# Heads as one pipeline with the gate inside, values stored through the input rows' buffers, and three engines kept in written order

## The chip, the core and the metric

The kernel runs on one core of a Trainium2 chip. The core has five engines that work side by side and meet through semaphores: PE (TensorE, the matrix products), DVE (VectorE), ACT (ScalarE), POOL (GpSimd) and SP (SyncE, which here issues the DMAs). The matrix products write to PSUM, of which this kernel uses eight banks of 128 x 512 float32; everything else works on SBUF. Each engine takes its instructions in the order in which they stand in its own queue, so an instruction that waits holds up all that stand behind it on that engine. The metric is the time of one execution on the device in microseconds (us), lower is better.

## The reference, cut to what matters

One encoder layer on x (1, 1024, 1024): a gMLP branch A, an attention branch B with eight heads of 128 and three dilated windows, two gates, an output product and a norm.

```
h = rms_norm(x, g_pre)
u_a, v_a, z_a, q_b, k_b, v_b, z_b, gate_a, gate_b = split(h @ w_in)
y_a = spatial_gating(gelu(u_a), gelu(v_a), ln_g, ln_b, w_s, b_s) * silu(z_a)
y_b = mixture_of_dilations(q_b, k_b, v_b) * silu(z_b)   # windows (128,1), (512,4), (2048,16)
m = sigmoid(gate_a) * (y_a @ w_pa) + sigmoid(gate_b) * (y_b @ w_pb)
out = x + rms_norm(m @ w_o, g_post)
```

## The kernel before

All products run in float32r as three matmuls, high by high, high by low and low by high. To get the two parts, ACT copies a tile (`wh_...`, `..h`) and DVE or POOL subtracts the copy from the source (`wl_...`, `..l`): `split` (L158) for activations, `operand` (L103) for weights.

The program has four stages. **Start** (L202 to L345): eight row tiles of x (`xt`, six buffers) are normed and transposed, and the values v_b are formed in two column blocks `cb` of 512. `v_out` (L249) splits each 128 x 512 bank of values into `vh` and `vl` and stores both to DRAM; `vh` lies in one of the two `ws` buffers, `vl` in one of two of its own. **Projections** (L347 to L575): all other columns of w_in, by a scheme with seven products for a 2 x 2 block (`seven`, L369); the sums of weight tiles that it needs are formed on DVE, the first two (`s1`, `s2`) in the same two `ws` buffers (`weight_operands`, L351, L364). The first of these groups are the gates `g0`, whose first product `g0p` needs no sum and whose second needs `s2`. The gating z_b goes to DRAM (`z_d`). **Attention** (L576 to L912): for each head `h`, `queries_keys` loads and splits q and k; `scores` makes 16 score tiles of 128 x 256 in eight pairs (`sc` banks, PE), DVE adds the bias and finds the row extreme in one instruction (L661, into `st` and `own`), and ACT takes the exponential with its sum (L665). `exchange` (L669) moves maxima and sums between partitions, half 0 on POOL and half 1 on DVE, 16 small copies each (`oth`). `normalise` (L682) makes the factors (`nm`), partly through an exponential on ACT (`dd`), and `scale` (L699) applies them to `st`. `weigh` (L712) then runs nine stages; each transposes scaled weights on PE (`pb`, `pa`, `pe` banks), splits them (`pth`, `ptl`), and, two stages later (`LAG` = 2), multiplies them with the values (`pr`, `pc` banks). After the ninth stage the last two are finished, the parts are added (L803) and the head's output goes to DRAM (`o_d`).

Between all this stand the products of branch A with w_pa, cut into 256 steps of three matmuls each (`mlp_products`, L834; banks `pa`, L857 to L859), which the loop over the heads deals out: `BESIDE` says how many steps follow each stage, `PAIRS` how many score pairs of the next head. **Tail** (L913 to L1014): `gated_heads` (L917) loads o and z of two heads at a time (two `o` buffers, one `z` buffer), POOL multiplies them, and the product is split into `yh`, `yl`; the steps that are left run beside it. Then come the products with w_pb (L977 to L979) and w_o (L1008 to L1010).

A scheduler decides the order in the engines' queues: it takes the written program as priorities and moves an instruction ahead when it finds it ready in its own estimate, buffers included.

Of the kernel before, what the change touches and what calls it, by code (L numbers as in the profile page):

```python
# [9 lines left out]
F32 = mybir.dt.float32  # L10
F32R = mybir.dt.float32r
# [12 lines left out]
H = 8  # L24
# [12 lines left out]
def tile_hybrid_encoder(  # L37
# [164 lines left out]
    with tc.tile_pool(name="start", bufs=1) as sp:  # L202
# [44 lines left out]
                transposed(hT[j][b], i, xs, f"xT{c}{j}")  # L247

        def v_out(c, cb, ps):  # L249
            vh = wpool.tile([P, 512], F32R, tag="ws", bufs=2, name=f"vh{cb}{c}")  # L250
            vl = sp.tile([P, 512], F32R, tag="vl", bufs=2, name=f"vl{cb}{c}")
            split(vh, vl, ps)
            for t, d in ((vh, v_hi), (vl, v_lo)):
                stored.append(nc.sync.dma_start(d[c * P:(c + 1) * P, 512 * cb:512 * (cb + 1)], f32(t)))
# [321 lines left out]
    with tc.tile_pool(name="heads", bufs=1) as hp, tc.tile_pool(name="attn", bufs=1) as ap:  # L576
        def queries_keys(h, res):

            def pair(nm, shape):
                return [hp.tile([P] + shape, F32R, tag=f"{nm}{s}", name=f"{nm}{s}{h}") for s in "hl"]  # L580

            res["qr"], res["qc"], res["kr"] = pair("qr", [4, 256]), pair("qc", [8, P]), pair("kr", [4, 256])
            for b in range(2):
                t = wpool.tile([P, 512], F32, tag="ws", bufs=2, name=f"q{h}{b}")
                nc.sync.dma_start(t, q_d[h][:, 512 * b:512 * (b + 1)])
                split(*[w[:, :, b * P:(b + 1) * P] for w in res["qr"]], t.rearrange("p (j r) -> p r j", r=4))
                split(*[w[:, 4 * b:4 * b + 4, :].rearrange("p a (r i) -> p a r i", r=4) for w in res["qc"]],
                      t.rearrange("p (a i r) -> p a r i", a=4, r=4), nc.gpsimd)
                yield
            for s in range(2):  # L590
                nc.sync.dma_start(f32(res["kr"][s]), k_d[h][:, s])
                yield
            for x, terms, shape in (("ta", alibi_a, [P, 256]), ("te", alibi_e, [P, 2, 192]), ("tb", alibi_b, [P, 384])):
                res[x] = hp.tile(shape, F32, tag=x, name=f"{x}{h}")
                nc.sync.dma_start(res[x], terms[h])

        def residue_values(h, res):

            res["vb"] = []
            for s, vd in enumerate((v_hi, v_lo)):  # L600
# [21 lines left out]
        def scores(h, res):  # L622
# [3 lines left out]
            qr, qc, kr, ta, te, tb = [res[n] for n in ("qr", "qc", "kr", "ta", "te", "tb")]  # L626
            own = res["own"] = hp.tile([P, 2, 8, 2], F32, tag="own", bufs=2, name=f"own{h}")
            wts = res["wts"] = {}
            order = [(1, (i, i + 1)) for i in (0, 2, 4, 6)] + [(0, (0, 7)), (0, (1, 2)), (0, (3, 4)), (0, (5, 6))]
            for half, pair in order:  # L630
                ps = bank("sc", f"sc{h}{half}{pair[0]}").rearrange("p (t n) -> p t n", t=2)
                st = (hp if half else ap).tile([P, 2, 256], F32, tag=f"st{half}", bufs=8 if half else 6, name=f"st{h}{half}{pair[0]}")
                n = 256
                for t, idx in enumerate(pair):
                    if half:
# [74 lines left out]
                                                           [(0, 5), (0, 6)], []]  # L710

        def weigh(h, res):  # L712


            va, ve, vb, wts = [res[n] for n in ("va", "ve", "vb", "wts")]
# [73 lines left out]
            for i, stage in enumerate([residue(r) for r in range(4)] + [chunk(1), chunk(3), ends(), chunk(5), chunk(7)]):  # L789
# [79 lines left out]
        ya = {}  # L869
        take(mlp_tiles(0, 0, ya))  # L870
        steps = mlp_products(ya)
        heads = [{} for _ in range(H + 1)]
        take(queries_keys(0, heads[0]))
        take(steps, 8)
        residue_values(0, heads[0])
        chunk_values(0, heads[0])
        for _ in scores(0, heads[0]):
            take(steps, 1)
        take(exchange(0, heads[0], 0))
        take(exchange(0, heads[0], 1))  # L880
        normalise(0, heads[0])
        for tile_ in TILES[0] + TILES[1]:
            scale(heads[0], *tile_)
        for _ in queries_keys(1, heads[1]):
            take(steps, 3)
        for h in range(H):
            more = h + 1 < H
            pairs = scores(h + 1, heads[h + 1]) if more else iter(())
            ahead = queries_keys(h + 2, heads[h + 2]) if h + 2 < H else iter(())
            for i, _ in enumerate(weigh(h, heads[h])):  # L890
                take(pairs, PAIRS[i])
                take(steps, BESIDE[i])
                if i == 3 and more:
                    residue_values(h + 1, heads[h + 1])
                if more and i == 3:
                    take(exchange(h + 1, heads[h + 1], 0))
                    late = exchange(h + 1, heads[h + 1], 1)
                if more and i in (5, 6):
                    take(late, 1)
                if more and i == 7:  # L900
                    normalise(h + 1, heads[h + 1])
                if more and i == 8:
                    for tile_ in TILES[0] + TILES[1]:
                        scale(heads[h + 1], *tile_)
                if i > 4:
                    take(ahead, 1)
            if more:
                chunk_values(h + 1, heads[h + 1])
            take(ahead)
            take(steps, BESIDE[9])  # L910


    with tc.tile_pool(name="tail", bufs=1) as tp:  # L913

        y = {}

        def gated_heads(h, b):  # L917

            bs = slice(512 * b, 512 * (b + 1))
            o, z = [tp.tile([P, 2, 512], F32, tag=t, bufs=n, name=f"{t}{h}{b}") for t, n in (("o", 2), ("z", 1))]  # L920
            for t, src in ((o, o_d), (z, z_d)):
                nc.sync.dma_start(t, src[h:h + 2, :, bs].rearrange("k p n -> p k n"))
            for i in range(2):
                y[h + i, b] = [tp.tile([P, 512], F32R, name=f"y{s}{h + i}{b}") for s in "hl"]
                nc.gpsimd.tensor_tensor(o[:, i, :], o[:, i, :], z[:, i, :], ALU.mult)  # L925
                split(*y[h + i, b], o[:, i, :])
                yield

        ready = (_ for h in range(0, H, 2) for b in range(2) for _ in gated_heads(h, b))
        wb = {}  # L930
        for i in range(16):
            take(ready, 1)
# [130 lines left out]
```

## Time and profile before

| | us |
|---|---|
| median of 3 runs | 1597.32 (1597.07 to 1600.4) |
| the profiled execution's own time | 1596.76 |
| its span in the trace | 1595.0 |
| PE busy | 1519.5 (95%) |
| DVE busy | 882.6 (55%) |
| POOL busy | 769.4 (48%) |
| ACT busy | 689.7 (43%) |
| start ends, projections begin | about 135 |
| first transpose of head 0 | 1059.6 |
| first transpose of head 7 | 1332.7 |
| first load of o in the tail | 1362.8 |

A row of a list of groups has the line and engine, what is written from what, the shape, the count, then the busy time, the mean of one in ns, and the idle time of the engine just before them with what ended it. A row of the timeline has the start, the duration, the engine and the instruction, and in brackets the idle time before it. A row of the windows has, for a stretch of the span, each engine's busy time and number of instructions, then the granted clock of PE as a share of full speed. PE's matmuls are pipelined: one is shown as 0.39 us long, and the next may start before it ends.

### The profile page before, as it was taken

What the parts mean: (1) busy time and instruction counts of PE and PEld (TensorE: products, weight loads), DVE (VectorE), ACT (ScalarE), POOL (GpSimd) and SP (SyncE); (2) the same over time, 40 slices, a digit from 0 to 9 for tenths busy, and PEclk for the clock granted to TensorE, in tenths of its full rate; (3) what the DMA queues carried; (4) which work ended last, traced back from release to release, by engine and by line L of the source; (5) the groups of instructions that cost most, each with busy time, mean ns of one, the idle gap of its engine ahead of it and who ended that gap; (6) DMA issues with size and microseconds to landing.
All of it is one profiled execution on the core that took longest, in us unless ns stands there. A gap on an engine that the chain in (4) does not pass through costs nothing. (4 is left out here: it accounts for less than half of the span.)

```text
span 1595.0 us, 22762 instructions
## 1 busy us (share of the span) xinstructions
PE 1519.5 (95%) x7863; PEld 1277.7 (80%) x7863; DVE 882.6 (55%) x1706; ACT 689.7 (43%) x1315; POOL 769.4 (48%) x703
## 2 busy tenths in 40 slices
PE   8998999999999999999999999989998989979998
PEld 4786999988888888788788888778787767758886
DVE  5723444476675665857564655577777575232112
ACT  5522433343433434343444444677766565221111
POOL 2413544465555555555555555454444443664132
PEclk9999999999999999999999999999999989989999
DMA  8445333334534443636344443586666657785531
GB/s 258 157 166 177 117 103 107 111 126 132 165 122 149 130 154 106 184 101 188 110 146 136 131 138 123 188 234 196 207 186 187 205 161 206 223 248 175 198 106 66
DMA packets 247812, 252.16 MB, mean 158 GB/s; under 512 B 14184, under 2 KB 187272, under 8 KB 247440
## 3 DMA queue, kind: packets, MB, share of 16 engines
q1 hardware_dynamic: 247328, 249.88, 49.9%
q8 instruction: 62, 1.02, 0.3%
q10 hardware_dynamic: 368, 0.82, 0.2%
q14 instruction: 54, 0.44, 0.1%
HBM read 174.10 MB, written 76.55 MB: 157 GB/s over the span
## 5 line engine op out<-in xcount | busy, mean ns | idle before, releaser
L108 POOL TENSOR_TENSOR wl_pa<-wr_pa,wh_pa 128x512 fp32r<-128x512 f32 x56 | 73.7, 1322 | 98.1 <-ACT wh_pa L106 89.5
L512 DVE TENSOR_SCALAR vn<-vn,mean,rstd 128x128 f32<-128x128 f32 x128 | 57.1, 500 | 35.1 <-DMA vn<-v_d 34.8
L665 ACT ACTIVATE st<-st,own 128x256 f32<-128x256 f32 (+1 forms) x128 | 62.9, 492 | 24.7 <-DVE own L661 24.3
L977 PE MATMUL pb<-yh,wh_pb 128*128 128x512 f32 x128 | 50.6, 396 | 10.2 <-ACT yh L159 10.2
L978 PE MATMUL pb<-yl,wh_pb 128*128 128x512 f32 x128 | 50.8, 397 | 1.5 <-DVE yl L160 1.4
L106 ACT ACTIVATE wh_pa<-wr_pa 128x512 fp32r<-128x512 f32 x64 | 38.9, 624 | 28.8 <-PE pa L858 16.0
L678 DVE COPY oth<-own 32x4 f32<-32x4 f32 x128 | 47.3, 369 | 5.6 <-ACT st L665 3.5
L979 PE MATMUL pb<-yh,wl_pb 128*128 128x512 f32 x128 | 50.3, 393 | 0.0
L678 POOL COPY oth<-own 32x4 f32<-32x4 f32 x128 | 27.2, 212 | 38.5 <-ACT st L665 33.5
L981 POOL TENSOR_TENSOR mb<-thb,mb 128x512 f32<-128x512 f32 x16 | 20.6, 1288 | 45.7 <-DVE thb L980 36.2
L1012 ACT ACTIVATE sq<-o 128x512 f32<-128x512 f32 x16 | 9.6, 598 | 74.6 <-PE o L1010 74.6
L160 POOL TENSOR_TENSOR vl<-vn,vh 128x512 fp32r<-128x512 f32 x32 | 41.3, 1290 | 0.8 <-ACT vh L159 0.8
L160 DVE TENSOR_TENSOR yl<-o,yh 128x512 fp32r<-128x512 f32 x16 | 18.2, 1135 | 39.4 <-ACT yh L159 38.7
L992 DVE TENSOR_TENSOR sso<-sso 128x1 f32<-128x1 f32 x8 | 1.3, 159 | 67.6 <-ACT sq L1012 67.6
L160 POOL TENSOR_TENSOR qcl<-q,qch 128x512 fp32r<-128x512 f32 x16 | 25.8, 1621 | 26.0 <-ACT qch L159 26.0
L977 PEld LDWEIGHTS pb<-yh,wh_pb 128*128 128x128 f32 x128 | 24.4, 191 | 16.1 <-ACT yh L159 11.0
L160 DVE TENSOR_TENSOR vl<-vb,vh 128x512 fp32r<-128x512 f32 x16 | 10.9, 688 | 44.0 <-ACT vh L159 36.2
L661 DVE CUSTOM_DVE_ANT_0 st<-sc,tb 128x256 f32<-128x256 f32 x64 | 24.9, 419 | 17.7 <-PE sc L660 10.3
L165 POOL TENSOR_TENSOR sso<-sso,mhalf 128x1 f32<-128x1 f32 x8 | 4.4, 550 | 59.1 <-DVE sso L164 59.1
L658 PE MATMUL sc<-krh,qch 128*128 128x256 f32 (+1 forms) x80 | 24.6, 309 | 8.2 <-DVE own L661 7.6
L108 POOL TENSOR_TENSOR wl_wos<-wr_wos,wh_wos 128x512 fp32r<-128x512 f32 x16 | 20.7, 1294 | 22.8 <-ACT wh_wos L106 22.8
L160 DVE TENSOR_TENSOR ptla<-pa,ptha 128x512 fp32r<-128x512 f32 (+1 forms) x32 | 19.8, 619 | 20.1 <-ACT ptha L159 19.9
(2640 smaller groups left out, 5857.3 us busy)
## 6 DMA issues: line engine op xcount, KB each, us to landing
wr_pa<-in_w_proj_a_dram SPq DMA_DIRECT2D x32, 512.0 KB, 5.1
wr_g<-in_w_in_dram SPq DMA_DIRECT2D x16, 512.0 KB, 3.6
wr_va<-in_w_in_dram SPq DMA_DIRECT2D x16, 512.0 KB, 3.7
wr_u<-in_w_in_dram SPq DMA_DIRECT2D x16, 512.0 KB, 4.4
wr_z<-in_w_in_dram SPq DMA_DIRECT2D x16, 512.0 KB, 4.3
vn<-v_d SPq DMA_DIRECT2D x32, 256.0 KB, 2.8
y_d<-s SPq DMA_DIRECT2D x32, 256.0 KB, 3.0
wr_yf<-y_d SPq DMA_DIRECT2D x16, 512.0 KB, 6.6
```

Of the source, the lines that this page charges most:

```text
L106: nc.scalar.activation(hi, src, AF.Copy)
L108: low.tensor_tensor(lo, src, f32(hi), ALU.subtract)
L160: low.tensor_tensor(lo, src, f32(hi), ALU.subtract)
L512: nc.vector.tensor_scalar(vn[:, c, :], vn[:, c, :], mean[:, 4 * b + c, 0:1], rstd[:, 4 * b + c:4 * b + c + 1], op0=ALU.subtract, op1=ALU.mult)
L658: nc.tensor.matmul(dst, lhs[0], rhs[0], start=True, stop=False)
L661: nc.vector.tensor_tensor_reduce(st[:, t, :n], ps[:, t, :n], bias, -1.0, -NEG, ALU.add, ALU.min, own[:, half, idx, 0:1])
L665: nc.scalar.activation(st[:, t, :n], st[:, t, :n], AF.Exp, bias=own[:, half, idx, 0:1], scale=-1.0, accum_out=own[:, half, idx, 1:2])
L678: (nc.gpsimd, nc.vector)[half].tensor_copy(dst, src)
L977: nc.tensor.matmul(ps, lh, rh, start=(k == 0), stop=False)
L978: nc.tensor.matmul(ps, lh, rl, start=False, stop=False)
L979: nc.tensor.matmul(ps, ll, rh, start=False, stop=(k == KT - 1))
L981: nc.gpsimd.tensor_tensor(ma, th, ma, ALU.add)
```

## The change

Four things are changed.

- In the start, the values of the second column block go into one tile of 128 x 2 x 512 in the `xt` buffers of the input rows, not into `ws` and `vl`.
- In the attention, the last two stages of a head are finished in the first two stages of the next head's loop, not at the end of its own; each stage takes its score pairs one by one between the steps; the pairs come in another order, `exchange` and `normalise` stand a stage later, and the steps per head go from 22 to 24.
- `weigh` also loads z of its head and POOL multiplies o with it before o is stored; the tail loads only the product and splits it, every other one with POOL.
- From the first head on, PE, DVE and ACT keep the order in which the program is written; POOL and SP are still placed by the scheduler. The score tiles `st` get 7 and 7 buffers, not 8 and 6.

```
 def v_out(c, cb, ps):
-    vh = wpool.tile([P, 512], F32R, tag="ws", bufs=2, name=f"vh{cb}{c}")
-    vl = sp.tile([P, 512], F32R, tag="vl", bufs=2, name=f"vl{cb}{c}")
+    if cb:
+        vhl = sp.tile([P, 2, 512], F32R, tag="xt", bufs=6, name=f"vhl{c}")
+        vh, vl = vhl[:, 0, :], vhl[:, 1, :]
+    else:
+        vh = wpool.tile([P, 512], F32R, tag="ws", bufs=2, name=f"vh{c}")
+        vl = sp.tile([P, 512], F32R, tag="vl", bufs=2, name=f"vl{c}")
...
-    order = [(1, (i, i + 1)) for i in (0, 2, 4, 6)] + [(0, (0, 7)), (0, (1, 2)), (0, (3, 4)), (0, (5, 6))]
+    order = [(1, (i, i + 1)) for i in (0, 2, 4, 6)] + [(0, (1, 2)), (0, (3, 4)), (0, (5, 6)), (0, (0, 7))]
...
 def weigh(h, res):
...
-            for stage in begun:
+            zs = []
+            for b in range(2):
+                zs.append(wpool.tile([P, 512], F32, tag="ws", bufs=2, name=f"zt{h}{b}"))
+                nc.sync.dma_start(zs[b], z_d[h][:, 512 * b:512 * (b + 1)])
+            for i, stage in enumerate(begun):
                 take(stage)
+                if i + 1 < len(begun):
+                    yield
             for b in range(2):
...
                 nc.vector.tensor_tensor(o4, po[b].rearrange("p (a r i) -> p a r i", a=4, r=4), o4, ALU.add)
+                nc.gpsimd.tensor_tensor(o[:, hs], o[:, hs], zs[b], ALU.mult)
                 nc.sync.dma_start(o_d[h][:, hs], o[:, hs])
+            yield
...
-PAIRS = (2, 2, 2, 2, 0, 0, 0, 0, 0)
-BESIDE = (2, 1, 1, 2, 1, 2, 3, 3, 3, 4)
+PAIRS = (2, 1, 2, 2, 0, 1, 0, 0, 0)
+BESIDE = (3, 2, 2, 3, 2, 3, 3, 3, 3)
...
+with tc.manual_schedule(engines={mybir.EngineType.PE, mybir.EngineType.DVE, mybir.EngineType.Activation}):
...
+    before = iter(())
     for h in range(H):
...
-        for i, _ in enumerate(weigh(h, heads[h])):
-            take(pairs, PAIRS[i])
-            take(steps, BESIDE[i])
+        stages = weigh(h, heads[h])
+        for i in range(9):
+            take(stages, 1)
+            take(before, 1)
+            for j in range(BESIDE[i]):
+                if j < PAIRS[i]:
+                    take(pairs, 1)
+                take(steps, 1)
...
-            if more and i in (5, 6):
+            if more and i in (6, 7):
                 take(late, 1)
-            if more and i == 7:
+            if more and i == 8:
                 normalise(h + 1, heads[h + 1])
...
+        before = stages
+    for _ in before:
+        take(steps, 3)
...
 # tail
-            for t, src in ((o, o_d), (z, z_d)):
-                nc.sync.dma_start(t, src[h:h + 2, :, bs].rearrange("k p n -> p k n"))
+            tag, n = (("o", 2), ("z", 1))[h // 2 % 3 == 2]
+            t = tp.tile([P, 2, 512], F32, tag=tag, bufs=n, name=f"yf{h}{b}")
+            nc.sync.dma_start(t, o_d[h:h + 2, :, 512 * b:512 * (b + 1)].rearrange("k p n -> p k n"))
             for i in range(2):
-                nc.gpsimd.tensor_tensor(o[:, i, :], o[:, i, :], z[:, i, :], ALU.mult)
-                split(*y[h + i, b], o[:, i, :])
+                split(*y[h + i, b], t[:, i, :], (nc.vector, nc.gpsimd)[i])
```

Three places show how the queues change. The first is DVE at the end of the start. Before, the two weight sums `ws_g0s1` and `ws_g0s2` stand behind the last splits `vl` of the values:

```order
L160 TENSOR_TENSOR t4l3_990<-t4T3_991,t4h3_989 128x512
L160 TENSOR_TENSOR vl10_1061<-vb10_0_920,vh10_1060 128x512
L160 TENSOR_TENSOR vl14_1067<-vb10_1_921,vh14_1066 128x512
L160 TENSOR_TENSOR vl11_1073<-vb10_2_922,vh11_1072 128x512
L160 TENSOR_TENSOR vl15_1079<-vb10_3_923,vh15_1078 128x512
L160 TENSOR_TENSOR vl12_1185<-vb12_0_1084,vh12_1184 128x512
L160 TENSOR_TENSOR vl16_1191<-vb12_1_1085,vh16_1190 128x512
L160 TENSOR_TENSOR vl13_1197<-vb12_2_1086,vh13_1196 128x512
L160 TENSOR_TENSOR vl17_1203<-vb12_3_1087,vh17_1202 128x512
L364 TENSOR_TENSOR ws_g0s1_1240<-wr_g00_1216,wr_g01_1218 128x512
L364 TENSOR_TENSOR ws_g0s2_1242<-ws_g0s1_1240,wr_g00_1216 128x512
```

In the changed kernel, on DVE at the same place (`vhl` are the value tiles in the rows' buffers):

```order
L368 TENSOR_TENSOR ws_g0s1_1232<-wr_g00_1208,wr_g01_1210 128x512
L368 TENSOR_TENSOR ws_g0s2_1234<-ws_g0s1_1232,wr_g00_1208 128x512
L160 TENSOR_TENSOR t3l_116<-t3T3_965,t3h_115 128x4x128
L160 TENSOR_TENSOR t1l_112<-t1T3_973,t1h_111 128x4x128
L160 TENSOR_TENSOR t2l_114<-t2T3_981,t2h_113 128x4x128
L160 TENSOR_TENSOR t4l3_990<-t4T3_991,t4h3_989 128x512
L160 TENSOR_TENSOR vhl0_1060<-vb10_0_920,vhl0_1060 128x512
L160 TENSOR_TENSOR vhl4_1065<-vb10_1_921,vhl4_1065 128x512
```

The two sums have moved ahead of all eight splits of the second column block.

The second place is DVE at the end of head 1, where head 2 is made ready. Before (`ptla15`, `ptla17` are splits of head 1's last stages, `qrl3` a split of head 3's queries, `oth2`, `nm2`, `dd2` the exchange and the factors of head 2):

```order
L661 ISA st205_10739,own2_10583<-sc205_10738,ta2_10545 128x256
L661 ISA own2_10583 128x1
L678 COPY oth2_10770<-own2_10583 32x2x2 x8
L688 TENSOR_TENSOR nm2_10932<-own2_10583,oth2_10770 128x16
L689 TENSOR_TENSOR dd2_10931<-nm2_10932,own2_10583 128x16
L690 TENSOR_TENSOR dd2_10931<-nm2_10932,oth2_10770 128x16
L863 TENSOR_TENSOR tha03_10804<-tha03_10804,pa03_10459 128x512
L692 TENSOR_TENSOR nm2_10932<-dd2_10931,own2_10583 128x16
L693 TENSOR_TENSOR dd2_10931<-dd2_10931,oth2_10770 128x16
L694 TENSOR_TENSOR nm2_10932<-nm2_10932,dd2_10931 128x16
L695 RECIPROCAL nm2_10932<-nm2_10932 128x16
L160 TENSOR_TENSOR ptla17_10947<-pa17_10943,ptha17_10946 128x256
```

In the changed kernel, on DVE at that place:

```order
L160 TENSOR_TENSOR qrl3_10871<-q30_10876,qrh3_10870 128x4x128
L160 TENSOR_TENSOR ptle1_10886<-pe1_10882,pthe1_10885 64x256
L682 COPY oth2_10776<-own2_10584 32x2x2 x8
L160 TENSOR_TENSOR qrl3_10871<-q31_10918,qrh3_10870 128x4x128
L160 TENSOR_TENSOR ptla15_10930<-pa15_10924,ptha15_10929 128x512
L682 COPY oth2_10776<-own2_10584 32x2x2 x8
L160 TENSOR_TENSOR ptla17_10971<-pa17_10967,ptha17_10970 128x256
L692 TENSOR_TENSOR nm2_10994<-own2_10584,oth2_10776 128x16
L693 TENSOR_TENSOR dd2_10993<-nm2_10994,own2_10584 128x16
```

All 16 copies now stand in the last three stages, between query splits, and the factors stand behind the split of the last stage.

The third place is PE there: what stands ahead of `pb20`, the first transposes of head 2, which read the scaled tiles `st210` and `st214`. Before, the two last products of head 1 (`pc11`) and twelve matmuls of steps (the last is shown) come first:

```order
L757 MATMUL pc11_10861<-ptha15_10900,va01_10525 128x256 x2
L757 MATMUL pc11_10861<-ptha15_10900,va11_10535 128x256 x2
L757 MATMUL pc11_10861<-ptla15_10901,va01_10525 128x256 x2
L757 MATMUL pc11_10861<-ptha17_10946,va01_10525 128x256
L757 MATMUL pc11_10861<-ptha17_10946,va11_10535 128x256
L757 MATMUL pc11_10861<-ptla17_10947,va01_10525 128x256
...
L859 MATMUL pa04_10927<-ya0111h_9683,wl_pa0401_10499 128x512
L723 MATMUL pb20_11032<-ident_69,st210_10585 128x128
L723 MATMUL pb20_11032<-ident_69,st214_10630 128x128
```

In the changed kernel, on PE at that place:

```order
L872 MATMUL pa05_10954<-ya0000h_9661,wl_pa0500_10478 128x512
L728 MATMUL pb20_11036<-ident_69,st210_10586 128x128
L728 MATMUL pb20_11036<-ident_69,st214_10639 128x128
L728 MATMUL pb20_11036<-ident_69,st210_10586 128x128
L728 MATMUL pb20_11036<-ident_69,st214_10639 128x128
L762 MATMUL pc11_10890<-ptha15_10929,va01_10535 128x256 x2
L762 MATMUL pc11_10890<-ptha15_10929,va11_10545 128x256 x2
L762 MATMUL pc11_10890<-ptla15_10930,va01_10535 128x256 x2
L662 MATMUL sc310_11058<-krh3_10874,qrh3_10870 128x256
```

The products of head 1's last two stages have moved behind head 2's first transposes, and the twelve step matmuls that stood ahead of these are gone from there.

More of the change, by code (lines that the diff above doesn't have):

```diff
@@ L628, in scores @@
             wts = res["wts"] = {}
-            order = [(1, (i, i + 1)) for i in (0, 2, 4, 6)] + [(0, (0, 7)), (0, (1, 2)), (0, (3, 4)), (0, (5, 6))]
+            order = [(1, (i, i + 1)) for i in (0, 2, 4, 6)] + [(0, (1, 2)), (0, (3, 4)), (0, (5, 6)), (0, (0, 7))]
             for half, pair in order:
                 ps = bank("sc", f"sc{h}{half}{pair[0]}").rearrange("p (t n) -> p t n", t=2)
-                st = (hp if half else ap).tile([P, 2, 256], F32, tag=f"st{half}", bufs=8 if half else 6, name=f"st{h}{half}{pair[0]}")
+                st = (hp if half else ap).tile([P, 2, 256], F32, tag=f"st{half}", bufs=7, name=f"st{h}{half}{pair[0]}")
                 n = 256
@@ L871, in tile_hybrid_encoder @@
         steps = mlp_products(ya)
[L872 to L889, printed above, removed]
-            for i, _ in enumerate(weigh(h, heads[h])):
-                take(pairs, PAIRS[i])
-                take(steps, BESIDE[i])
[L893 to L897, printed above, removed]
-                if more and i in (5, 6):
-                    take(late, 1)
-                if more and i == 7:
[L901 to L910, printed above, removed]
+        with tc.manual_schedule(engines={mybir.EngineType.PE, mybir.EngineType.DVE, mybir.EngineType.Activation}):
+            heads = [{} for _ in range(H + 1)]
+            take(queries_keys(0, heads[0]))
+            take(steps, 8)
+            residue_values(0, heads[0])
+            chunk_values(0, heads[0])
+            for _ in scores(0, heads[0]):
+                take(steps, 1)
+            take(exchange(0, heads[0], 0))
+            take(exchange(0, heads[0], 1))
+            normalise(0, heads[0])
+            for tile_ in TILES[0] + TILES[1]:
+                scale(heads[0], *tile_)
+            for _ in queries_keys(1, heads[1]):
+                take(steps, 3)
+            before = iter(())
+            for h in range(H):
+                more = h + 1 < H
+                pairs = scores(h + 1, heads[h + 1]) if more else iter(())
+                ahead = queries_keys(h + 2, heads[h + 2]) if h + 2 < H else iter(())
+                stages = weigh(h, heads[h])
[5 more added lines that the diff above has]
+                            take(pairs, 1)
+                        take(steps, 1)
+                    if i == 3 and more:
+                        residue_values(h + 1, heads[h + 1])
+                        take(exchange(h + 1, heads[h + 1], 0))
+                        late = exchange(h + 1, heads[h + 1], 1)
+                    if more and i in (6, 7):
+                        take(late, 1)
+                    if more and i == 8:
+                        normalise(h + 1, heads[h + 1])
+                        for tile_ in TILES[0] + TILES[1]:
+                            scale(heads[h + 1], *tile_)
+                        chunk_values(h + 1, heads[h + 1])
+                    if i > 4:
+                        take(ahead, 1)
+                take(ahead)
+                before = stages
+            for _ in before:
+                take(steps, 3)
@@ L913, in tile_hybrid_encoder, with load_heads @@
     with tc.tile_pool(name="tail", bufs=1) as tp:
         y = {}
-        def gated_heads(h, b):
-            bs = slice(512 * b, 512 * (b + 1))
-            o, z = [tp.tile([P, 2, 512], F32, tag=t, bufs=n, name=f"{t}{h}{b}") for t, n in (("o", 2), ("z", 1))]
-            for t, src in ((o, o_d), (z, z_d)):
-                nc.sync.dma_start(t, src[h:h + 2, :, bs].rearrange("k p n -> p k n"))
+        def load_heads(h, b):
+            tag, n = (("o", 2), ("z", 1))[h // 2 % 3 == 2]
+            t = tp.tile([P, 2, 512], F32, tag=tag, bufs=n, name=f"yf{h}{b}")
+            nc.sync.dma_start(t, o_d[h:h + 2, :, 512 * b:512 * (b + 1)].rearrange("k p n -> p k n"))
@@ L923, in gated_heads @@
             for i in range(2):
                 y[h + i, b] = [tp.tile([P, 512], F32R, name=f"y{s}{h + i}{b}") for s in "hl"]
-                nc.gpsimd.tensor_tensor(o[:, i, :], o[:, i, :], z[:, i, :], ALU.mult)
-                split(*y[h + i, b], o[:, i, :])
+                split(*y[h + i, b], t[:, i, :], (nc.vector, nc.gpsimd)[i])
                 yield
-        ready = (_ for h in range(0, H, 2) for b in range(2) for _ in gated_heads(h, b))
+        ready = (_ for h in range(0, H, 2) for b in range(2) for _ in load_heads(h, b))
```

## The prediction

> **What bounds the kernel now.** I read the page's busy times first, then the list of what PE waited for, then PE's busy time and granted clock by stretch, and last the timeline where those waits lie.
>
> ```profile
> PE 1519.5 (95%) x7863; PEld 1277.7 (80%) x7863; DVE 882.6 (55%) x1706; ACT 689.7 (43%) x1315; POOL 769.4 (48%) x703
> ```
>
> PE is busy for all but 75.5 us of the span, and the change takes no product away. So the time can fall only by what PE waits, and by what it does at a lower clock. The waits, longest sum first (us in total, times, longest):
>
> ```profile
> PE sc L658 <- DVE own L661: 11.8, 11, 2.6
> PE pb L977 <- ACT yh L159: 10.2, 1, 10.2
> PE g0p L408 <- ACT wh_g0p L106: 6.0, 1, 6.0
> PE pc L757 <- ACT ptha L159: 5.3, 4, 2.8
> PE pc L757 <- DVE ptla L160: 4.3, 4, 2.9
> PE pb L723 <- DVE st L704: 3.5, 2, 3.3
> ```
>
> One lies at the end of the start (g0p), one in the tail (pb from yh), the rest in the attention. The stretches (length, then busy time of PE, PE's weight loads, DVE, ACT, POOL, then the clock) put lengths to them; the edges between 1059.6 and 1332.7 are the first transposes of heads 0 to 7:
>
> ```profile
> 135.00:155.00 20.00, 13.78 (x48) 10.35 (x48) 10.32 (x12) 7.62 (x14) 10.40 (x8) 0.83 0.79 283
> 1059.60:1105.50 45.90, 42.42 (x219) 35.58 (x220) 33.19 (x89) 32.69 (x76) 26.74 (x35) 0.85 0.70 216
> 1141.10:1175.10 34.00, 32.73 (x208) 28.27 (x207) 25.22 (x78) 24.49 (x61) 16.74 (x27) 1.00 0.69 207
> 1252.80:1300.00 47.20, 39.72 (x217) 32.51 (x216) 29.75 (x80) 26.79 (x65) 20.62 (x30) 0.89 0.65 194
> 1300.00:1332.70 32.70, 31.11 (x198) 26.90 (x197) 21.98 (x77) 20.10 (x57) 9.45 (x23) 1.00 0.57 168
> 1357.00:1402.00 45.00, 41.92 (x183) 33.79 (x182) 14.00 (x14) 13.02 (x22) 30.75 (x23) 1.00 0.75 224
> 1402.00:1432.00 30.00, 18.45 (x71) 13.72 (x71) 10.72 (x14) 8.15 (x14) 17.61 (x14) 0.83 0.78 243
> ```
>
> A head that runs undisturbed takes 34.0 us (1141.1 to 1175.1) with DVE and ACT busy for 25 of them. The seven from 1059.6 to 1332.7 take 273.1, against 7 x 34.0 = 238.0: 35.1 us are lost, most of it in few heads (the first, 45.9, and the one of 47.2), where the clock is below 1.
>
> **The start.** PE's last product of g0p and the next ones, DVE's rows about them, and when the weights were fetched:
>
> ```profile
> 137.32 0.39 PE L410 MATMUL g0p<-hT00l,wh_g0p 128*128 128x512 f32 x1
> 137.55 0.39 PE L412 MATMUL g0p<-hT00h,wl_g0p 128*128 128x512 f32 x1
> 143.90 0.79 PE L408 MATMUL g0p<-t2h,wh_g0p 128*128 128x512 f32 x1 [5.97 <-ACT wh_g0p L106]
> 146.39 0.63 PE L410 MATMUL g0p<-t2l,wh_g0p 128*128 128x512 f32 x1
> 146.82 0.63 PE L412 MATMUL g0p<-t2h,wl_g0p 128*128 128x512 f32 x1
> 138.88 0.69 DVE L160 TENSOR_TENSOR vl<-vb,vh 128x512 fp32r<-128x512 f32 x1 [3.66 <-DMA vb_l<-vl]
> 140.57 0.68 DVE L364 TENSOR_TENSOR ws_g0s<-wr_g,wr_g 128x512 f32<-128x512 f32 x1
> 142.44 0.69 DVE L364 TENSOR_TENSOR ws_g0s<-ws_g0s,wr_g 128x512 f32<-128x512 f32 x1 [1.19 <-DMA vb_h<-vh]
> 80.60 5.81 SPq L113 DMA_DIRECT2D wr_g<-in_w_in_dram  x2
> 99.12 0.69 DVE L160 TENSOR_TENSOR t3l<-t3T,t3h 128x512 fp32r<-128x512 f32 x1 [6.03 <-ACT t3h L159]
> ```
>
> The sums wait for stores of values that hold the `ws` and `vl` buffers (3.66 and 1.19 us), PE waits 5.97, and then its first twelve matmuls start 0.43 us apart (146.39, 146.82) where it had been 0.23 (137.32, 137.55): 12 x 0.20 = 2.4, and some 0.6 more for the slower first ones, so about 9 us. In the changed order the sums stand ahead of the splits of the second block; their weights were issued by 86.4, and DVE has a hole of 6.03 us ahead of 99.12. What is late next is the copy of g0p's bank into a tile in memory that the start's stores still hold: PE does 12 x 0.23 = 2.8 us of other products meanwhile, and I leave 0.5. Term: **-8.5** (from 0, if some other store holds it, to -9).
>
> **The tail.** The waits there are 45.00 - 41.92 = 3.1 and 30.00 - 18.45 = 11.5 us, and at a clock of 0.83 over the second stretch I put 2 us on top: 16.6.
>
> ```profile
> L925 POOL TENSOR_TENSOR o<-o,z x16: 1260/1290/1731, 1369.4 to 1419.5; 128x512 f32<-128x512 f32 x16
> L922 SPq DMA_DIRECT2D z<-z_d x8: 359/360/462, 1363.2 to 1413.2; - x8
> DMA to landing us min/median/max: 5.9/5.9/5.9
> ```
>
> Eight loads of z go through one buffer from 1363.2 to 1413.2, 7.1 us apart: 5.9 to land, then POOL's two products of 1.29. In the change the products are made in the attention, only o is loaded, and the eight loads share three buffers, so none has more than three loads one behind the other: 3 x (5.9 + 2.6) = 26 us at most. Beside that PE still has 256 - 28 - 8 x 24 = 36 steps, 30 of them behind the last head: 30 x 3 x 0.23 = 21 us, and the first product with w_pb needs the last head only after 5 us more. The store is later by two gate products, 2.6 us. I leave 5 us of wait. Term: **-11.5** (from -16.6 to 0).
>
> **The heads.** Moved steps are no gain: PE does them anyway. Where a head's last transposes and the `pc` products of their split had 21 PE instructions between them, they now have 50, so the 9.6 us of waits on `ptha` and `ptla` should go. In exchange PE meets the next head's scaled tiles sooner. PE, DVE and POOL at that place in the undisturbed head:
>
> ```profile
> 1163.02 0.60 PE L723 MATMUL pa<-ident,st 128*128 128x128 f32 x4
> 1163.93 0.39 PE L658 MATMUL sc<-krh,qch 128*128 128x256 f32 x1
> 1164.40 0.56 PE L757 MATMUL pc<-ptha,va 128*128 128x128 f32 x4
> 1170.57 0.64 PE L757 MATMUL pc<-ptha,va 128*128 128x256 f32 x4
> 1175.09 0.38 PE L723 MATMUL pb<-ident,st 128*128 128x128 f32 x2
> 1124.36 0.16 DVE L678 COPY oth<-own 32x4 f32<-32x4 f32 x1
> 1164.35 0.69 DVE L160 TENSOR_TENSOR ptla<-pa,ptha 128x512 fp32r<-128x512 f32 x1 [0.48 <-ACT ptha L159]
> 1165.41 4.09 DVE L678 COPY oth<-own 32x4 f32<-32x4 f32 x8
> 1171.98 1.17 DVE L704 TENSOR_SCALAR st<-st,nm 128x256 f32<-128x256 f32 x3
> 1165.90 3.04 POOL L160 TENSOR_TENSOR qcl<-q,qch 128x512 fp32r<-128x512 f32 x2 [0.87 <-ACT qch L159]
> 1164.71 2.14 ACT L159 ACTIVATE qch<-q 128x512 fp32r<-128x512 f32 x2
> ```
>
> From the transposes of the last but one stage (1163.02) to `pb` (1175.09) PE has 12.1 us of work; DVE's chain (split, eight copies, factors, first two scales) ends 0.39 behind 1171.98, 9.3 us after the same start, and `pb` finds its tiles ready. In the changed order PE has only what lies from 1163.02 to 1170.57, less the score products from 1163.93 to 1164.40 that now stand elsewhere: 7.1 us. So with DVE as it was, PE waits 2.2 us at each of seven boundaries. Two things move that wait. The eight copies took 4.09 us because POOL's two qcl ran in them; free of POOL, as at 1124.36, they take 8 x 0.16 = 1.3, and the wait is nothing. And eight more copies and both query splits, each behind ACT's 1.07 us copies, now stand just ahead on a queue that keeps its order: the chain can start late by as much again. I take 3 us, near the row, and 1.5 for the clock that a wait of this size costs here:
>
> ```profile
> 1288.14 0.41 PE L723 MATMUL pa<-ident,st 128*128 128x128 f32 x2 [3.30 <-DVE ptle L160]
> 1289.89 0.63 PE L858 MATMUL pa<-ya1310l,wh_pa 128*128 128x512 f32 x1
> ```
>
> After 3.30 us without work the matmuls took 0.63, not 0.39. The Trainium skill ("TensorE: Matmul & The Clock Gate", HAM oscillation — how this bites in real kernels) says that only idle gaps over about 3.4 us halve the clock. By that rule my boundaries would cost 3 us and the sum would be 10 us lower, 1560; the trace shows the slow matmuls already behind 3.30 us, so the row decides.
>
> So a head costs 34.0 - 0.6 (its own wait for `ptla`) + 4.5 = 3.9 us above the best one: 7 x 3.9 = 27.3 against 35.1 now, **-7.8** (bounds: -35 with no wait, +27 with 9.5 at each). The two heads that also split activations of the other branch keep part of their excess, since ACT and DVE now meet those splits in fixed places: **+4**. Ahead of head 0 PE has 39 matmuls (9.0 us) between its last scores and `pb`, before 23 (5.3): its wait of 3.3 goes, **-3**.
>
> The rest I cost at nothing. The two gate products of each head, 2 x 1.29 on POOL, stand in its second stage beside score reductions that read PSUM; POOL is busy for 16.74 of 34.0. Behind them on POOL stand the copies of half 0 and weight splits; if z came late, these would too, but the steps' operands are made seven ahead. The 16 small z loads take SP 0.36 each, ahead of a weight load that has two buffers in reserve. Fewer `st` buffers of half 1 only require the tile seven before, read by the transposes two stages earlier.
>
> **Sum**, against the profiled execution's 1596.8 (0.6 under the median): -8.5 - 11.5 - 7.8 + 4 - 3 = -26.8, so 1570.
>
> **Rivals.**
> - *No wait at the boundary.* POOL's work falls elsewhere, the copies take 1.3 us, the chain ends before PE comes: 7 x 4.5 = 31 less, 1539. For it: free of POOL a copy takes 0.16 us. Against it: POOL's queue in these stages holds two query splits and up to four weight splits.
> - *Slower: copies held by POOL.* If both groups of eight copies meet a POOL that goes from one product to the next, each product of 1.3 to 1.5 us lets one copy through; the row above shows two such (4.09 us). With five in line the chain ends 5 us later than I took, PE idles 8 us and its clock falls: 9.5 a boundary, 7 x 5 = 35 more, 1605. It decides from about four such products per boundary. The Trainium skill ("SBUF — State Buffer", Who interferes with whom) says that a VectorE copy or scale of this kind and a GpSimd instruction shut each other out for the whole instruction. By that rule the gate products, new in the attention, speak against the change; the trace agrees that copies stretch, and no run here shows the gates there.
> - *The ends don't give.* The sums or the o loads find another store or buffer in their way: half of 20 us stays, 1580.
>
> **How the numbers follow.** My forecast 0.50 (1556 to 1591), no wait 0.22 (1530 to 1553), held copies 0.18 (1592 to 1615), weak ends 0.10 (1572 to 1593). Leaving out a tenth at each side gives 1541 to 1602. A measurement of this kernel tells 0.2% from no change, 1594.1 to 1600.5: faster 0.82, same 0.06, slower 0.12, the last from the upper half of the held copies.
>
> **What would show it.** Right: no wait of g0p on wh_g0p; the first product with w_pb without its 10 us; waits of `pb` on `st` (L708) seven times, 2 to 4 us each, and none of `pc` on `ptha`. Wrong: those waits missing (first rival) or over 6 us with rows of copies over 5 us (second); a wait of a weight product for a raw tile, since ACT now holds its place for it; heads longer than 45 us.

## The result and the profile after

The changed kernel took **1696.1 us** (median of 4 runs, 1694.4 to 1698.7) where the kernel before took 1597.2 beside it: a ratio of 1.062, 95% interval 1.060 to 1.064. It is 99 us slower. The forecast was 1570, range 1541 to 1602, with 0.82 on faster. It was wrong, in sign and by far.

The profiled execution has a span of 1692.9 us, 97.9 above the one before. The first part of its page, busy time by engine:

```profile
PE 1554.9 (92%) x7863; PEld 1305.1 (77%) x7863; DVE 876.5 (52%) x1698; ACT 696.6 (41%) x1315; POOL 773.7 (46%) x711
```

The same 7863 matmuls keep PE busy 35.4 us longer (1554.9 against 1519.5), and it stands still 62.5 us more (138.0 against 75.5). So nearly two thirds of the loss is waiting; the rest is matmuls that take longer, most of it at a lower clock (granted in the mean 0.960, against 0.982 before). The list of PE's waits in the changed kernel (us in total, times, longest), as read before:

```profile
PE sc L662 <- DVE own L665: 78.5, 64, 11.5
PE pb L728 <- DVE st L708: 30.6, 7, 9.6
PE g0p L412 <- ACT g0u L388: 2.6, 1, 2.6
PE pb L994 <- ACT yh L159: 1.9, 1, 1.9
```

The row of the score products on a reduction had 11 waits and 11.8 us before. It now has 64, one for each pair of score tiles (8 heads of 8 pairs), and 78.5 us. The two rows that the forecast wanted gone are gone or small (g0p on its weight 6.0, now 2.6 on something else; pb on yh 10.2, now 1.9), and the seven waits of first transposes that it foresaw are there. By stretch (length, busy time of PE, its weight loads, DVE, ACT, POOL, then the clock):

```profile
135.00:155.00 20.00, 17.36 (x77) 14.07 (x76) 10.12 (x12) 7.12 (x12) 7.01 (x5) 1.00 0.84 292
1085.36:1133.04 47.68, 35.54 (x205) 29.68 (x203) 27.44 (x76) 26.23 (x62) 20.59 (x30) 0.96 0.47 146
1133.04:1184.48 51.44, 41.02 (x213) 34.19 (x213) 27.99 (x80) 25.62 (x60) 18.27 (x29) 0.87 0.52 153
1232.04:1289.67 57.63, 41.02 (x212) 34.20 (x213) 31.78 (x82) 28.72 (x66) 22.00 (x32) 0.83 0.52 153
1289.67:1350.06 60.39, 44.12 (x212) 36.66 (x213) 31.19 (x84) 30.80 (x70) 24.93 (x34) 0.81 0.59 178
1451.88:1512.49 60.61, 57.10 (x293) 47.66 (x293) 18.21 (x30) 24.82 (x46) 34.55 (x27) 1.00 0.64 196
```

The edges from 1085.36 to 1451.88 are again the first transposes of heads 0 to 7. The seven heads between them take 366.5 us, 52.4 each, against 273.1 before: 93.4 more. What lies ahead of head 0's first transposes is 25.8 us longer (1085.4 against 1059.6), and what lies behind head 7's is 21.3 shorter (1692.9 - 1451.9 = 241.0 against 1595.0 - 1332.7 = 262.3). 93.4 + 25.8 - 21.3 = 97.9, the whole difference. **The ends gained; the attention lost over a hundred.**

What a wait of the large row is, on PE's timeline early in head 1, where the scores of head 2 are made, and on DVE's:

```profile
1135.22 0.41 PE L662 MATMUL sc<-krh,qrh 128*128 128x256 f32 x1
1135.44 0.41 PE L663 MATMUL sc<-krl,qrh 128*128 128x256 f32 x1
1135.65 0.41 PE L664 MATMUL sc<-krh,qrl 128*128 128x256 f32 x1
1136.59 0.58 PE L662 MATMUL sc<-krh,qrh 128*128 128x256 f32 x1 [0.52 <-DVE own L665]
1136.10 0.42 DVE L665 CUSTOM_DVE_ANT_0 st<-sc,tb 128x256 f32<-128x256 f32 x1
1136.45 0.08 DVE L665 DVE_READ_ACCUMULATOR2_ANT own<- 128x1 f32 x1
```

Three products fill the first half of a score bank, DVE reduces that half (end 1136.53), and only then do the products of the second half of the same bank start. In the code the reduction of half 0 stands ahead of the products of half 1, and both halves are parts of one tile, so the program makes the second half wait. That was so before, too. But there the scheduler had put other work in between; the same place in the undisturbed head of before (head 2, with the scores of head 3):

```profile
1141.42 0.36 PE L658 MATMUL sc<-krh,qrh 128*128 128x256 f32 x1
...
1141.86 0.28 PE L658 MATMUL sc<-krh,qrh 128*128 128x256 f32 x1
...
1142.22 0.40 PE L857 MATMUL pa<-ya0000h,wh_pa 128*128 128x512 f32 x1
1142.45 0.40 PE L858 MATMUL pa<-ya0000l,wh_pa 128*128 128x512 f32 x1
1142.69 0.28 PE L658 MATMUL sc<-krh,qrh 128*128 128x256 f32 x1
```

Six score products follow each other without a wait, so they are halves of two different banks; step products come before the next half. In written order the second half follows at once, 64 times.

### The profile page after: what moved, and what is told of

Same layout as the page of the kernel before. It is cut to its first block, busy times and chain, and to the rows that moved or that the text cites. A ratio compares the mean times of both kernels' runs of the same rounds, so it can differ in the third digit from the quotient of the medians.

```text
span 1692.9 us, 22772 instructions
## 1 busy us (share of the span) xinstructions
PE 1554.9 (92%) x7863; PEld 1305.1 (77%) x7863; DVE 876.5 (52%) x1698; ACT 696.6 (41%) x1315; POOL 773.7 (46%) x711
## 4 chain that ended last, share of the span: by engine, by line
PE 68%; DVE 11%; issue 6%; DMA 5%; POOL 3%; ACT 3%; SPq 1%; ACTq 0%; POOLq 0%; DVEq 0%
PE pa L870 2%; PE pa L871 2%; DVE oth L682 2%; PE pa L872 2%; PE pb L994 2%; PE sc L662 2%; PE pb L995 2%; PE pb L996 2%; DMA wr_pa<-in_w_proj_a_dram 2%; PE sg L527 1%; PE vb L154 1%; PE vb L155 1%; PE vb L156 1%; DVE st L665 1%; POOL out L1015 1%
## 5 line engine op out<-in xcount | busy, mean ns | idle before, releaser
L662 PE MATMUL sc<-krh,qrh 128*128 128x256 f32 x64 | 26.8, 419 | 55.3 <-DVE own L665 55.3
L516 DVE TENSOR_SCALAR vn<-vn,mean,rstd 128x128 f32<-128x128 f32 x128 | 57.2, 501 | 35.2 <-DMA vn<-v_d 34.9
L662 PEld LDWEIGHTS sc<-krh,qrh 128*128 128x128 f32 x64 | 15.8, 248 | 64.1 <-DVE own L665 63.1
L815 POOL TENSOR_TENSOR o<-o,zt 128x512 f32<-128x512 f32 x16 | 20.2, 1279 | 75.9 <-DVE o L814 75.9
L682 DVE COPY oth<-own 32x4 f32<-32x4 f32 x128 | 53.5, 418 | 1.9 <-ACT st L669 0.2
L728 PE MATMUL pb<-ident,st 128*128 128x128 f32 x128 | 24.5, 314 | 31.0 <-DVE st L708 30.6
L160 DVE TENSOR_TENSOR ptlb<-pb,pthb 128x512 fp32r<-128x512 f32 x32 | 22.1, 691 | 53.3 <-ACT pthb L159 53.3
L728 PEld LDWEIGHTS pb<-ident,st 128*128 128x128 f32 x128 | 18.6, 163 | 39.9 <-issue 34.8
L662 PE MATMUL sc<-krh,qch 128*128 128x256 f32 (+2 forms) x80 | 25.2, 315 | 23.2 <-DVE own L665 23.2
L662 PEld LDWEIGHTS sc<-krh,qch 128*128 128x128 f32 x80 | 15.5, 194 | 30.2 <-DVE own L665 29.4
L682 POOL COPY oth<-own 32x4 f32<-32x4 f32 x128 | 23.5, 183 | 33.1 <-ACT st L669 19.7
```

The costliest lines, as they stand in the source:

```text
L160: low.tensor_tensor(lo, src, f32(hi), ALU.subtract)
L516: nc.vector.tensor_scalar(vn[:, c, :], vn[:, c, :], mean[:, 4 * b + c, 0:1], rstd[:, 4 * b + c:4 * b + c + 1], op0=ALU.subtract, op1=ALU.mult)
L662: nc.tensor.matmul(dst, lhs[0], rhs[0], start=True, stop=False)
L682: (nc.gpsimd, nc.vector)[half].tensor_copy(dst, src)
L728: nc.tensor.transpose(pt[:n, c0:c0 + P], src, ident)
```

## The experiments

Theory A: the halves of a pair, exposed by PE's written order, are most of the loss, directly and through the clock. Rival B: VectorE and ScalarE in written order are the bound, and the wait on the reduction only shows how late they are. Rival C: not the order, but the gates or the new stages in the attention.

| run | what it is | us (median) | ratio to before, 95% |
|---|---|---|---|
| pair_apart | changed; both halves' products ahead of both reductions | 1616.4 | 1.011 [1.009, 1.013] |
| free_all | changed; no written order | 1576.1 | 0.986 [0.984, 0.988] |
| hold_pe | changed; written order on PE alone | 1628.0 (one run) | |
| hold_dve_act | changed; written order on DVE and ACT alone | 1651.1 (one run) | |
| hold_pe_pair | hold_pe with the halves as in pair_apart | 1574.5 | 0.986 [0.984, 0.987] |
| free_pair | free_all with the halves as in pair_apart | 1568.7 | 0.983 [0.981, 0.985] |
| pair_early | pair_apart; exchange and factors a stage sooner | 1598.0 | 1.001 [1.000, 1.002] |
| late_hold | pair_early; written order only behind head 0's preparation | 1585.8 | 0.994 [0.991, 0.996] |
| before_vout | before; with the values' new buffers alone | 1590.0 | 0.996 [0.995, 0.997] |
| before_pair | before; with the halves as in pair_apart | 1587.6 | 0.994 [0.991, 0.996] |
| tail_back | free_pair; gates and z loads back in the tail | 1575.3 | 0.986 [0.983, 0.988] |
| free_pair_turn | free_pair; banks of the transposes alternate across heads | 1567.2 | 0.981 [0.978, 0.983] |

**The halves alone (pair_apart).**

```diff
                         nc.tensor.matmul(dst, lhs[1], rhs[0], start=False, stop=True)
-                    nc.vector.tensor_tensor_reduce(st[:, t, :n], ps[:, t, :n], bias, ...
+                    todo.append((t, idx, n, bias))
+                for t, idx, n, bias in todo:
+                    nc.vector.tensor_tensor_reduce(st[:, t, :n], ps[:, t, :n], bias, ...
```

> Theory A (the two halves of a score pair share a bank, the second half's products wait until the reduction of the first is done, and the written order of PE leaves nothing between them): with both halves' products ahead of both reductions the 51 waits under 1 us (29.6 us in all, some 10 more for the refill of PE) and most of the eight of 2.7 to 3.2 us go, and PE's clock rises with them: 1696 falls to 1640 (1625 to 1655). The two long waits ahead of head 0 (11.5 and 8.9 us) and the waits of the first transposes of heads 1 to 7 (30.6 us) stay. Rival B (VectorE and ScalarE in written order are the bound, the wait on the reduction only shows their lateness): the time is found again in other waits, 1680 or more.

Measured 1616.4: 79.7 us come back, more than A asked for, and B is out as the main cause. The page's row and the two largest waits:

```profile
PE 1520.0 (94%) x7863; PEld 1287.0 (80%) x7863; DVE 865.4 (54%) x1698; ACT 685.7 (42%) x1315; POOL 778.1 (48%) x711
```

```profile
PE pb L731 <- DVE st L711: 38.2, 7, 10.5
PE sc L663 <- DVE own L668: 19.2, 3, 9.2
```

Of the 64 waits three are left, two of them the long ones ahead of head 0 (8.5 and 9.2). PE's idle time falls by 41.1 us (138.0 to 96.9) and its busy time by 34.9; the second is what A had sized too low. Not all of it is the clock: the mean granted clock rises from 0.960 to 0.971, so the share lost to it, times the span, falls from 67.7 to 46.9 us, by 21. Another 10 to 12 us is an estimate from the rows above: a product shown as 0.41 us lets the next start 0.22 behind it (0.28 and 0.12 in the rows of before), so at each of 61 waits 0.16 to 0.19 us counts as busy that lies under the next product elsewhere. The clock in the changed kernel behind a boundary wait of 3.57 us, then in this run behind one of 4.04 us:

```profile
1133.04:1135.04 2.00, 1.91 (x10) 1.72 (x11) 1.38 (x4) 0.60 (x1) 1.41 (x2) 0.66 0.12 32
1135.04:1143.04 8.00, 6.95 (x23) 5.59 (x23) 2.78 (x11) 2.41 (x8) 0.00 (x0) 0.50 0.22 63
1143.04:1145.04 2.00, 1.93 (x12) 1.52 (x10) 0.05 (x1) 0.60 (x1) 0.00 (x0) 0.78 0.00 0
```

```profile
1119.49:1123.49 4.00, 3.91 (x18) 3.62 (x19) 2.76 (x7) 0.60 (x1) 1.41 (x2) 0.58 0.26 68
1123.49:1129.50 6.01, 6.01 (x40) 5.32 (x39) 3.38 (x13) 2.79 (x9) 0.27 (x1) 0.99 0.39 105
```

In these rows the clock stays at 0.50 for 8 us with half-microsecond waits between the pairs, and without them it is back in four. That the short waits hold it down is not shown. The first row below, of the changed kernel, begins 4 us behind a wait of 3.46 us: the clock is back at 1.00, with a wait of 0.53 us just ahead of the row and one of 0.52 in it. The second, of the kernel before, begins at the end of a wait of 2.35 us: the clock is at 0.50 for 6 us, and PE does not stand still in them.

```profile
1188.48:1192.48 4.00, 3.48 (x21) 2.86 (x21) 1.30 (x6) 2.13 (x8) 0.00 (x0) 1.00 0.03 7
1091.98:1097.98 6.00, 6.00 (x19) 5.16 (x20) 3.87 (x13) 3.23 (x6) 3.06 (x2) 0.50 0.85 274
```

The Trainium skill ("TensorE: Matmul & The Clock Gate", A second HAM failure mode: psum-queue depth-cycling) says that many short idles of PE between groups of matmuls can make its clock fall again and again. No run here shows that by itself: hold_pe, below, has all 64 waits and a mean clock of 0.980, against 0.982 before.

**The written order, engine by engine (free_all, hold_pe, hold_dve_act).**

```diff
-        with tc.manual_schedule(engines={PE, DVE, Activation}):
+        if True:                                                   # free_all
+        with tc.manual_schedule(engines={PE}):                     # hold_pe
+        with tc.manual_schedule(engines={DVE, Activation}):        # hold_dve_act
```

> The order of all engines is the scheduler's again, everything else as changed. Theory A and rival B both: 1575 (1555 to 1595), since the start and the tail keep their gains and score halves are put apart again. Rival C (the gates in the attention, or the new stages of exchange and factors, cost the time, not the written order): 1640 or more.

> Only PE keeps the written order. Theory A: the short waits of the second halves stay (some 40 us with the refill), the long waits ahead of head 0 go (20 us) and part of the boundary waits: 1655 (1640 to 1675). Rival B: with VectorE and ScalarE free most of the loss goes, under 1620.

> Only VectorE and ScalarE keep the written order, PE's is the scheduler's, which puts other products between the halves (64 single halves in its order, none in the written one). Theory A: 1615 (1595 to 1635). Rival B: the loss stays, 1670 or more.

Without the written order the change is **faster than before by 1.4%**, and rival C falls: gates, z loads and the later exchange are all in free_all, where they cost no such time. PE's row for the scores, in free_all and then in hold_pe:

```profile
PE sc L662 <- DVE own L665: 8.0, 7, 2.4
```

```profile
PE sc L662 <- DVE own L665: 58.7, 64, 3.3
```

PE's written order alone brings the 64 waits, with VectorE and ScalarE free. The long ones ahead of head 0 (11.5 and 8.9 us) are not among them, so these belong to the other two engines' order. hold_pe came out 27 us faster than A said (one run), hold_dve_act 36 slower (one run): A was right on the halves and had nothing for the rest. With DVE and ACT in the written order and PE scheduled:

```profile
PE pb L728 <- DVE st L708: 22.4, 8, 8.4
PE pc L762 <- DVE ptla L160: 16.7, 6, 4.2
PE pa L870 <- ACT ya0310h L159: 9.1, 2, 7.0
...
PE sc L662 <- DVE own L665: 2.8, 6, 0.5
```

The halves cost 2.8 us here, and the time goes into waits for splits and scaled tiles instead. That PE's scheduled order and the other engines' written one do not fit each other is how I read these rows. So a smaller form of B holds: fixed places of DVE and ACT can cost time apart from the halves, here 75 us above free_all.

**The halves with PE alone held, and with nothing held (hold_pe_pair, free_pair).**

> PE alone in the written order, VectorE and ScalarE scheduled, and both halves' products ahead of both reductions. Theory A: the 64 waits of hold_pe (58.7 us, some 10 more for the refill) go: 1560 (1550 to 1575). Rival B, with the engines' own orders against PE's: the time turns up at the transposes and the products behind them, 1590 or more.

> All engines scheduled, and both halves' products ahead of both reductions. Where the scheduler had already put other work between the halves there is little to gain: its seven waits of scores on a reduction were 8.0 us in all, so 1568 to 1577; faster than 1560 would say that the halves cost the scheduler more than its waits show.

The first took 1574.5 (A: 1550 to 1575, B: 1590 or more), 53.6 us under hold_pe, and of the row of scores on a reduction one wait of 0.4 is left. What it has in its place is 15.5 us of first transposes and two waits for data that came late in this one execution (10.9 on ya0310h, 10.5 on the keys of one head). free_pair took 1568.7, inside what was expected: the scheduler had hidden most halves, not all. Between 1574.5 and 1568.7 the intervals overlap.

**The halves in the kernel before (before_pair).**

> The kernel before with both halves' products ahead of both reductions, nothing else. The scheduler there had put other work between most halves: its 11 waits on a reduction were 11.8 us, 15.2 with the refill, of which the change to free_all recovered 7.4: 1589 (1584 to 1594). 1596 would say that the waits only move.

Measured 1587.6, 8 us faster than before by the medians (6.5 to 14 by the interval), as expected. The halves were a cost in the old kernel as well. Six waits of scores on a reduction stay (4.9 us, from 11 and 11.8), so not all eleven need have been halves.

**The boundaries, and head 0 (pair_early, late_hold).**

```diff
-                    if more and i in (6, 7):
+                    if more and i in (5, 6):
                         take(late, 1)
-                    if more and i == 8:
+                    if more and i == 7:
                         normalise(h + 1, heads[h + 1])
+                    if more and i == 8:
                         for tile_ in TILES[0] + TILES[1]:
```

> The written order of all three engines, both halves' products ahead of both reductions, and the exchange and the factors one stage sooner, as the kernel before had them. If the waits of the first transposes of heads 1 to 7 (38.2 us in pair_apart) come from VectorE's chain standing too close to them, a stage of 3 steps and 9 to 12 products (some 4 us) more cover takes five of them (4 us each) away and shortens the two of 10 us: 1616 falls to 1590 (1583 to 1600). If they come from the operands of ScalarE that wait for loads, little changes: 1608 or more.

> As pair_early, but the written order of the three engines begins behind head 0's scores, factors and the splits for head 1; up to there the scheduler orders. If the two long waits of PE ahead of head 0 (7.7 and 9.6 us, with 2.2 behind them) come from VectorE and ScalarE holding places for splits whose loads are late, they go, with some 2 us of refill: 1598 falls to 1577 (1570 to 1584). If the load itself is what PE's products need there, the wait shows as one of a product with w_proj_a for its activations: 1590 or more.

pair_early took 1598.0, 18.4 less, late_hold another 12.2 less. The first lies in the range expected for a chain too close to the boundary (1583 to 1600), at its upper end; the second falls between what was set against each other. Their rows, pair_early first:

```profile
PE pb L731 <- DVE st L711: 26.3, 6, 9.5
PE sc L663 <- DVE own L668: 21.6, 3, 9.6
```

```profile
PE pb L731 <- DVE st L711: 31.0, 7, 9.4
PE sc L663 <- DVE own L668: 6.3, 4, 3.7
```

A stage more cover took 1 to 2 us off each of the plain boundaries (3.9 to 4.3 before it, 2.0 to 3.3 with it) and 1.1 and 2.8 off the two of over 10, which stand where activations of the other branch are split. In late_hold the two long waits ahead of head 0 are gone, but a wait of 5.1 us of head 0's first transposes on a scaled tile and 2.8 us of step products on an activation come in, which suggests that the loads there are partly late by themselves. What ACT does ahead of the boundary with the longest wait (9.6 us) in the changed kernel, then DVE and POOL:

```profile
1280.07 0.63 ACT L106 ACTIVATE wh_pa<-wr_pa 128x512 fp32r<-128x512 f32 x1 [4.12 <-DMA wr_pa<-in_w_proj_a_dram]
1280.60 0.61 ACT L159 ACTIVATE ya1000h<-wr_yf 128x512 fp32r<-128x512 f32 x1
1281.12 0.36 ACT L159 ACTIVATE ptha<-pa 128x256 fp32r<-128x256 f32 x1
```

```profile
1281.05 5.38 DVE L682 COPY oth<-own 32x4 f32<-32x4 f32 x8
1286.47 0.42 DVE L160 TENSOR_TENSOR ptla<-pa,ptha 128x256 fp32r<-128x256 f32 x1
```

```profile
1280.78 1.27 POOL L108 TENSOR_TENSOR wl_pa<-wr_pa,wh_pa 128x512 fp32r<-128x512 f32 x1 [3.10 <-ACT wh_pa L106]
1282.00 1.27 POOL L160 TENSOR_TENSOR ya1000l<-wr_yf,ya1000h 128x512 fp32r<-128x512 f32 x1
1283.23 1.26 POOL L108 TENSOR_TENSOR wl_pa<-wr_pa,wh_pa 128x512 fp32r<-128x512 f32 x1
1284.44 1.26 POOL L160 TENSOR_TENSOR ya1111l<-wr_yf,ya1111h 128x512 fp32r<-128x512 f32 x1
```

ACT holds the place of a weight's split for 4.12 us while its load lands, and the copy of the transposes (ptha) stands behind it. But DVE does not wait for it: DVE works from 1273.44 to 1287.8 without standing still, and ptha is long done when DVE comes to its split. What delays DVE is its own 16 copies, 3.78 and 5.38 us for eight each, where eight take 1.3 undisturbed. ACT's wait is seen again on POOL: its weight split starts 3.10 us late, and four products in a row fall beside the second eight copies. So the late load may reach PE through POOL and the copies; no run shows this by itself.

**The start and the tail by themselves (before_vout, tail_back).**

> The kernel before with the change's buffers for the second block of values alone. My term for the start was 8.5 us: 1588.7 by that. By the losses of PE from 135 to 155 us in the traces of before and after (9.3 and 2.9 us) the change removes 6.4: 1590.8. If the wait is only moved to another buffer: 1597.

> As free_pair, with the gates and the loads of z back in the tail as the kernel before has them. My term for the tail was 11.5 us: 1569 rises to 1580. By the loss of PE behind 1357 us in the traces of before (some 17) and of after (7) it is 10: 1579. If the gates cost as much in the attention as they save in the tail (POOL is one engine), the time stays within 3 us of 1569.

The start is worth 5.9 us (4.5 to 8.5 by the interval). The tail is worth 6.5 by the medians, 8.3 us of waits on yh against 1.7 in the profiles; the two intervals of the ratio overlap, so its size is known only roughly.

**Alternating the banks across heads (free_pair_turn).**

```diff
-            pr, turn = {}, ["tp", "sc"]
+            pr = {}
```

The list `turn` is made once, outside the heads.

> As free_pair, with the alternation of the two banks of the transposes carried on from head to head. A head has nine stages, so its last and the next one's first use the same single bank, and five first transposes wait 15.6 us for the split of the last stage to empty it. Carried on, these waits go, with up to 5 us of refill and clock: 1569 falls to 1555 (1548 to 1562). If VectorE's chain to the scaled tiles ends no sooner, they come back as waits on the scaled tile: 1565 or more.

The medians differ by 1.5 us and the intervals overlap: no gain that can be told. The waits of first transposes on a split fell from 15.6 us (5) to 7.0 (2), but PE's idle time only from 57.9 to 53.9, and its busy time rose by 5.6: other waits came in, 3.3 and 2.2 us of `pc` on splits among them. The expected 14 us were wrong. The second case of the expectation held in its time (1565 or more) but not in its reason: the waits on a scaled tile went only from 4.7 to 5.6. With 1567 to 1569 us, 1.7 to 1.9% below before, it and free_pair are the fastest of all: the change without its written order, with the halves' products together.

## Why the prediction was wrong

One path through the runs accounts for the distance from 1696 to 1569: halves -79.7 (1616.4), exchange a stage sooner -18.4 (1598.0), head 0's preparation scheduled -12.2 (1585.8), the rest scheduled -17.0 (1568.7). The last step also puts the exchange back a stage later, so it is not the scheduling alone. The first step alone is four fifths of the 99 us.

- **The step that failed is the sentence "Moved steps are no gain: PE does them anyway", with "The rest I cost at nothing" behind it.** It priced what moves by its own busy time only. The steps' second service was to fill PE's time between the two halves of a pair, and the written order took them from there. The row that showed the price, 11 waits of scores on a reduction, 11.8 us, stood first in my own list and was never followed: why 11 and not 64? The others were covered by work that the scheduler had put between. With the halves apart, 79.7 us came back.
- **The boundary wait was foreseen; its size and its clock were too small.** I took 3 us of wait and 1.5 of clock at each of seven, and 4 more for the two heads with splits of the other branch. The waits are 3.4 to 3.8 at four of them, 9.6 and 5.3 at the two with such splits, 1.4 at the last: 30.6 in all. The clock cost 1.5 behind one of the four plain ones, as taken; behind the three others its mean was 0.53 to 0.57 over the next 11 to 12 us, some 4.6 us each (an estimate: PE's busy time there times the share lost).
- **The rival of held copies was half right.** Rows of copies over 5 us do appear (5.38 above, 5.66 ahead of a plain boundary), and two boundaries with over 5 us of wait. It lay at 1605, and with the halves repaired the kernel is at 1616. But it did not decide the result: a part of those 1616 is head 0 (19.2 us of waits), and the halves cost 80 us on top.
- **Ahead of head 0 I had 3 us of gain; PE waits 20.4 us there instead** (11.5 and 8.9). The wait of 3.3 for the first transposes did go. But head 0's score reductions now stand in DVE's queue behind splits that wait for ACT, and ACT waits for raw tiles, up to 5.4 us at a time. Such a wait had been named as a sign of error, and I had costed written order on ScalarE at nothing.
- **The start was mis-sized**: 8.5 foreseen, 5.9 measured (8.5 is the edge of the interval). I left 0.5 us for the copy of g0p's bank; it is 2.64:

```profile
145.19 0.50 PE L412 MATMUL g0p<-hT10h,wh_g0p 128*128 128x512 f32 x1 [2.64 <-ACT g0u L388]
```

- **The tail was mis-sized**: 11.5 foreseen, about 6.5 measured. The wait of 10.2 did go to 1.9, as said; but with the gates back in the tail of an otherwise improved kernel (tail_back) the waits are only 8.3 in six pieces. The loads of z lay 7.1 us apart, too, not the 5.9 + 2.6 that I counted for each.
- **Without the written order the sum comes out near, in part by luck.** free_all is 1576.1, 21.1 under before, where I had 26.8: start 5.9, tail about 6.5, heads about 8.7 by the difference. I had 6.8 for the heads with the first head's wait, but added up for fixed boundaries, with 4.5 us at each of seven. In free_all first transposes wait twice for a scaled tile, 2.7 us in all, and five times for a split, 11.5: other waits than those I had summed. No wait of `pc` on `ptha` is left in the changed kernel, as foreseen.

What stays open: how the last 17.0 us divide between DVE's and ACT's fixed places, PE's and the exchange, and how much of the wait ahead of head 0 is the loads' own lateness.

## What to carry to other kernels

Before you fix an order by hand, ask of every pair of dependent instructions that you write next to each other what the scheduler had put between them: a short list of waits in a scheduled trace shows what was left uncovered, not how many such pairs there are. Where several products and their readers share one tile, write all products first; that was worth 80 us in the fixed order and 8 even in the scheduled one. Fix one engine's order at a time and look, since orders of different origin (two engines fixed, one scheduled) can cost as much as the fault that one is after.

## What the runs showed of the hardware

Behind a PE wait of 3.57 us the granted clock was 0.50 for 8 us; behind one of 3.46 it was back at 1.00 after 4; behind one of 2.35, in the kernel before, it was 0.50 for 6 us without any wait in between. So in these traces the length of a wait does not say how long the clock stays low. Sixty-four waits of at most 3.3 us left the mean clock of hold_pe at 0.980. Removing 41.1 us of idle time took another 34.9 of busy time away, of which at most 21 is the clock. And the eight small copies of DVE, 0.16 us each when POOL is idle, took 5.38 us beside four of POOL's products.
